# Second MLP product as seven products of quarter matrices in a two-layer streaming encoder

## The chip, the cores and the metric

The kernel runs on one core of a Trainium2 chip. The metric is the device time of one execution in microseconds (us).

## The reference

Input and output are 1024 tokens of 1024 channels, float32. Two layers; each is a token mixer (differential attention in layer 0, a gated linear recurrence in layer 1) and an MLP with squared ReLU, both behind an RMSNorm and added to the residual; a last RMSNorm ends the trunk.

```python
def rmsnorm(x, g, eps=NORM_EPS):
    y = x * lax.rsqrt(jnp.mean(x * x, axis=-1, keepdims=True) + eps)
    return y * g

def sqrelu_mlp(h, w1, w2):
    return jnp.square(jax.nn.relu(h @ w1)) @ w2

for layer in range(DEPTH):
    ...
    x = x + sqrelu_mlp(rmsnorm(x, mlp_norm_g[layer]), mlp_w1[layer], mlp_w2[layer])
return rmsnorm(x, final_norm_g)
```

`w1` is 1024 x 4096, `w2` 4096 x 1024 (`D_FF` = 4096).

## The kernel before, in words

Activations lie with channels on the partitions and tokens along the free axis (tiles of 128 x 1024, two halves of `CH` = 512 tokens); there are 8 such blocks of `x`. Each factor of a product is split into a high part (fp32r, a copy on ScalarE) and a low part (the difference, on VectorE or GpSimd, in `split`, L91), and each product is three matmuls: high by high, high by low, low by high, of 128 x 128 weights by 512 columns (`mm3`, `gemm_steps`, `hidden_pair`).

**First MLP product.** `mlp` runs 16 times `hidden_pair`, each for two blocks of 128 hidden channels (`ct`, top, and `cl`, low). A pair is one step of Strassen's scheme as changed by Winograd: seven products A11·B11, A12·B21, S2·T2, S3·T3, S1·T1, S4·B22, A22·T4, each 4 x 3 = 12 matmuls, 84 in all. The sums of token and channel blocks (T1 to T4 and the parts of x) are split once ahead; those of the weights (`s12`, `s34`) in `pair_weights`, one pair ahead: three high parts (`wth`, `wsh` twice) and a half one (`wl`) on ScalarE, the low ones on VectorE (`wsl`, `wl`) and GpSimd (`wtl`, L91). The seven results lie in seven PSUM banks (`acb`; `acg` twice; two tiles `acc` of two banks each, tag S with two buffers) and VectorE adds them up (L808, `mt`, `ct`, `cl`). `finish` multiplies both blocks by 1/rms on GpSimd (L840), applies relu and square on ScalarE and stores the block in DRAM (`hid`). It runs one pair later. The 1/rms comes from the sum of squares `ssacc` (`norm_later`; its columns are made in pair 1, since the norm is only applied to the product).

**Second MLP product.** `mlp` then walks `GROUPS`, five groups of 4, 8, 8, 8 and 4 hidden blocks. A group loads and splits its blocks (`hidden_load`) and weights (`w_out`), and `out_group` multiplies them into each of the 8 output blocks and adds the result to the residual `x` (L739). That is 32 hidden blocks x 8 x 2 halves x 3 = 1536 matmuls in a layer. In layer 1 the last group is `final_group`: tokens as rows, `x` transposed on TensorE (64 of them, L908), final norm and output.

The order of the instructions on each engine is set by the scheduler of the language, from the order of the code and its own estimates; the buffers (`BUFS`: 46 of tag T, 4 of R and W) bound how far it may reach.

Of the kernel before, what the change touches and what calls it, by code (L numbers as in the profile page):

```python
# [9 lines left out]
F32 = mybir.dt.float32  # L10
# [31 lines left out]
class Trunk:  # L42
    def __init__(self, ctx, tc, ins, out):
# [9 lines left out]
        self.w_lo = None  # L53

# [250 lines left out]
    def gemm_steps(self, w, xs, sel, evict, tag=None):  # L305
# [456 lines left out]
    def pair_weights(self, w1, i):  # L762
# [9 lines left out]
        th, tl = self.split(top, (P, NK, P), "wt", "W" if i else "T", lo_eng=nc.gpsimd)  # L772
# [7 lines left out]
        h12, l12 = self.split(s12, (P, NK, P), "ws")  # L780
# [5 lines left out]
    def hidden_pair(self, w, i, rb, before):  # L786
# [7 lines left out]
        steps = (("A11", "B11"), ("A12", "B21"), ("S2", "T2"), ("S3", "T3"), ("S1", "T1"), ("S4", "B22"), ("A22", "T4"))  # L794
# [3 lines left out]
        banks = (p1, p2, p67[:, l], p67[:, r], p53[:, l], p53[:, r], p4)  # L798

        def product(n, k, first, last):  # L800
            a, b = steps[n]
            (ah, al), (bh, bl) = w[a], self.sx[k][b]
            mm(banks[n], ah[:, k], bh, start=first, stop=False)  # L803
            mm(banks[n], ah[:, k], bl, start=False, stop=False)  # L804
            mm(banks[n], al[:, k], bh, start=False, stop=last)  # L805
# [4 lines left out]
        t = self.t4("mt")  # L810
        top, low = self.t4("ct"), self.t4("cl")
        u2, u3 = t[:, l], t[:, r]

        def done(n):
            if n == 0:
                nc.scalar.activation(out=u2, in_=p1, func=AF.Copy)
            elif n == 1:
                add(top[:, l], u2, p2)
            elif n == 2:
                add(u2, u2, banks[2])  # L820
            elif n == 3:
# [9 lines left out]
        for n in range(7):
            for k in range(4):
                product(n, k, k == 0, k == 3)
            done(n)
            if n in before:
                before[n]()

        def finish():
# [16 lines left out]
    def mlp(self, layer, done, last):  # L855
# [5 lines left out]
        for i in range(16):  # L861
# [9 lines left out]
            if i:  # L871
                finish()
# [297 lines left out]
```

## Time and profile before

| | us |
|---|---|
| median of 3 runs (2367.36 to 2368.62) | 2368.48 |
| profiled execution | 2370.26 |
| its span | 2368.5 |
| TensorE busy | 2231.6 (94%) |
| VectorE busy | 1390.9 (59%) |
| ScalarE busy | 955.5 (40%) |
| GpSimd busy | 531.8 (22%) |

The granted clock over the span is 0.974 of full speed. A matmul's busy time is its whole passage, so 884 of them in 200 us stand as 200 us of busy time. The first product of layer 0 lies at about 640 to 970 us of the span, its second product up to some 1320, then the recurrence; layer 1's MLP fills the span from about 1680 on.

### The profile page before, as it was taken

What the parts mean: (1) busy time and instruction counts of PE and PEld (TensorE: products, weight loads), DVE (VectorE), ACT (ScalarE), POOL (GpSimd) and SP (SyncE); (2) the same over time, 40 slices, a digit from 0 to 9 for tenths busy, and PEclk for the clock granted to TensorE, in tenths of its full rate; (3) what the DMA queues carried; (4) which work ended last, traced back from release to release, by engine and by line L of the source; (5) the groups of instructions that cost most, each with busy time, mean ns of one, the idle gap of its engine ahead of it and who ended that gap; (6) DMA issues with size and microseconds to landing.
All of it is one profiled execution on the core that took longest, in us unless ns stands there. A gap on an engine that the chain in (4) does not pass through costs nothing.

```text
span 2368.5 us, 26083 instructions
## 1 busy us (share of the span) xinstructions
PE 2231.6 (94%) x10206; PEld 1838.3 (78%) x10206; DVE 1390.9 (59%) x1639; ACT 955.5 (40%) x1466; POOL 531.8 (22%) x323
## 2 busy tenths in 40 slices
PE   8998889788979999999999998989699999999998
PEld 7776777676768888888888877867588888888887
DVE  5327667665877777632223576778967777422224
ACT  5225556464544444421111354554444444311114
POOL 3011112110345444511100000001544445301000
PEclk9999999998989999999999999989899999999999
DMA  6434445643513333743321111113133335633211
GB/s 192 132 89 111 107 111 126 176 114 91 188 63 115 108 115 107 252 139 98 98 63 49 59 42 30 45 45 107 45 98 115 108 107 174 220 104 95 78 51 72
DMA packets 222525, 250.92 MB, mean 106 GB/s; under 512 B 10209, under 2 KB 180290, under 8 KB 222402
## 3 DMA queue, kind: packets, MB, share of 16 engines
q1 hardware_dynamic: 213570, 221.99, 29.3%
q0 software_dynamic: 7680, 25.17, 4.6%
q8 instruction: 80, 1.31, 0.2%
q10 hardware_dynamic: 1152, 2.10, 0.2%
q14 instruction: 43, 0.35, 0.0%
HBM read 157.99 MB, written 57.67 MB: 91 GB/s over the span
## 4 chain that ended last, share of the span: by engine, by line
PE 60%; DVE 7%; ACT 3%; issue 1%; POOLq 0%; ACTq 0%; DVEq 0%
PE acc L325 8%; PE acc L326 8%; PE acc L328 7%; PE acc L803 5%; PE acc L804 5%; PE acc L805 5%; PE acg L328 3%; PE acg L326 3%; PE acg L325 3%; PE acg L803 2%; PE acg L804 2%; PE acg L805 2%; DVE t L255 1%; PE acb L804 1%; PE acb L805 1%
## 5 line engine op out<-in xcount | busy, mean ns | idle before, releaser
L325 PE MATMUL acc<-hh,woh 128*128 128x512 f32 x648 | 252.1, 389 | 0.0
L326 PE MATMUL acc<-hl,woh 128*128 128x512 f32 x648 | 252.1, 389 | 0.0
L739 DVE TENSOR_TENSOR x<-x,acc 128x1024 f32<-128x1024 f32 x69 | 83.8, 1216 | 236.1 <-PE acc L328 236.0
L328 PE MATMUL acc<-hh,wol 128*128 128x512 f32 x648 | 199.5, 389 | 0.0
L88 ACT ACTIVATE woh<-raw 128x1024 fp32r<-128x1024 f32 x76 | 80.4, 1058 | 278.2 <-PE acc L326 187.8
L91 POOL TENSOR_TENSOR wtl<-raw,wth 128x1024 fp32r<-128x1024 f32 x32 | 89.0, 2783 | 322.7 <-ACT wth L88 314.1
L91 POOL TENSOR_TENSOR hl<-raw,hh 128x1024 fp32r<-128x1024 f32 x32 | 81.4, 2546 | 348.4 <-ACT hh L88 348.3
L482 ACT ACTIVATE p<-acc,nmax 128x768 f32<-128x768 f32 (+7 forms) x128 | 95.3, 744 | 153.9 <-DVE nmax L499 56.4
L88 ACT ACTIVATE hh<-raw 128x1024 fp32r<-128x1024 f32 x64 | 66.6, 1056 | 188.9 <-DMA raw<-hid 178.2
L328 PEld LDWEIGHTS acc<-hh,wol 128*128 128x128 f32 x648 | 121.6, 188 | 25.4
L325 PEld LDWEIGHTS acc<-hh,woh 128*128 128x128 f32 x648 | 121.6, 188 | 25.2
L326 PEld LDWEIGHTS acc<-hl,woh 128*128 128x128 f32 x648 | 121.6, 188 | 25.2
L840 POOL TENSOR_TENSOR ct<-ct,rstdb 128x1024 f32<-128x1024 f32 x32 | 106.6, 3333 | 128.7 <-DVE ct L808 100.3
L325 PE MATMUL acg<-xgh,wh 128*128 128x512 f32 x320 | 135.3, 423 | 0.0
L840 POOL TENSOR_TENSOR cl<-cl,rstdb 128x1024 f32<-128x1024 f32 x32 | 88.8, 2774 | 178.0 <-DVE cl L808 109.1
L164 POOL TENSOR_TENSOR rstd<-ms,mhalf 128x4 f32<-128x4 f32 (+2 forms) x27 | 28.3, 1047 | 444.5 <-DVE ms L162 423.4
L328 PE MATMUL acg<-xgh,wl 128*128 128x512 f32 x320 | 127.7, 399 | 0.4 <-DVE wl L91 0.4
L326 PE MATMUL acg<-xgl,wh 128*128 128x512 f32 x320 | 127.2, 398 | 0.0
L325 PE MATMUL acg<-hh,woh 128*128 128x512 f32 x312 | 121.4, 389 | 0.0
L328 PE MATMUL acg<-hh,wol 128*128 128x512 f32 x312 | 121.4, 389 | 0.0
L326 PE MATMUL acg<-hl,woh 128*128 128x512 f32 x312 | 121.4, 389 | 0.0
L91 DVE TENSOR_TENSOR wol<-raw,woh 128x1024 fp32r<-128x1024 f32 x76 | 101.3, 1333 | 29.5 <-ACT woh L88 29.5
(328 smaller groups left out, 5888.2 us busy)
## 6 DMA issues: line engine op xcount, KB each, us to landing
raw<-in_mlp_w_dram SPq DMA_DIRECT2D x128, 512.0 KB, 4.2
raw<-hid SPq DMA_DIRECT2D x64, 512.0 KB, 3.3
x<-x SPq DMA_DIRECT2D x32, 512.0 KB, 5.0
hid<-ct SPq DMA_DIRECT2D x32, 512.0 KB, 2.6
hid<-cl SPq DMA_DIRECT2D x32, 512.0 KB, 8.2
raw<-in_attn_w_qkv_dram SPq DMA_DIRECT2D x24, 512.0 KB, 4.2
ks<-qkh POOLq DMA_DIRECT2D x32, 256.0 KB, 6.4
ks<-qkl POOLq DMA_DIRECT2D x32, 256.0 KB, 6.5
```

The costliest lines, as they stand in the source:

```text
L88: nc.scalar.activation(out=hi, in_=src, func=AF.Copy)
L91: (lo_eng or nc.vector).tensor_tensor(out=lo, in0=src, in1=hi.bitcast(F32), op=ALU.subtract)
L164: nc.gpsimd.tensor_tensor(out=r, in0=ms, in1=self.mhalf[:, :w], op=ALU.pow)
L325: mm(ps[:, pc], a, xh[:, cs], start=(k == 0), stop=False)
L326: mm(ps[:, pc], a, xl[:, cs], start=False, stop=False)
L328: mm(ps[:, pc], b, xh[:, cs], start=False, stop=(k == n - 1))
L482: nc.scalar.activation(out=p[c][:, :n], in_=src, func=AF.Exp, bias=nmax[:, c : c + 1], accum_out=sums[:, c : c + 1])
L739: nc.vector.tensor_tensor(out=self.x[m][:, cs], in0=self.x[m][:, cs], in1=ps, op=ALU.add)
L803: mm(banks[n], ah[:, k], bh, start=first, stop=False)
L804: mm(banks[n], ah[:, k], bl, start=False, stop=False)
L805: mm(banks[n], al[:, k], bh, start=False, stop=last)
L840: nc.gpsimd.tensor_tensor(out=c, in0=c, in1=rb(), op=ALU.mult)
```

## The change

The second product also becomes one Strassen step. The hidden matrix and `w2` are taken as 2 x 2 quarters; there are seven products of quarters, and each is accumulated in PSUM over its whole length of 16 hidden blocks (`second`). It is written as 56 slots of 24 matmuls: 8 P, 16 A, 16 B, 8 C and 8 D, 1344 matmuls in a layer. A and B slots work on two products at once. `load` runs `AHEAD` = 4 slots before use, `prepare` (the splits and the sums of weights) one slot before, `after` reads finished banks, and `side` holds steps of VectorE that are spread over later slots. The order on TensorE, ScalarE, VectorE and the DMA queue is that of the code there (`manual_schedule`).

`hidden_pair` takes its seven products in another order, keeps the sums in `ct` and `cl` without `mt`, and makes the four half-block sums that the second product needs (`h12`, `h34`, L840 of the new file) on VectorE; a pair stores seven half-blocks in DRAM. The factor 1/rms leaves the hidden blocks: since relu and square follow, its square (1/(mean + eps), `inv`) multiplies the result. `wtl` moves from GpSimd to VectorE. In layer 1 `turn_x` transposes `x` in pairs 3 to 10, tokens are rows in the whole second product, and `final_part` does the last norm half by half.

```diff
-        th, tl = self.split(top, (P, NK, P), "wt", "W" if i else "T", lo_eng=nc.gpsimd)
...
+        th, tl = self.split(top, (P, NK, P), "wt", hi_tag="W")
...
-        steps = (("A11", "B11"), ("A12", "B21"), ("S2", "T2"), ("S3", "T3"), ("S1", "T1"), ("S4", "B22"), ("A22", "T4"))
...
-            for c in (top, low):
-                nc.gpsimd.tensor_tensor(out=c, in0=c, in1=rb(), op=ALU.mult)
...
+        product("A11", "B11", p1)
+        nc.scalar.activation(out=top[:, l], in_=p1, func=AF.Copy)
+        product("S2", "T2", p67[:, l])
+        add(low[:, l], top[:, l], p67[:, l])
+        product("S1", "T1", p53[:, l])
+        add(low[:, r], low[:, l], p53[:, l])
+        product("S4", "B22", p53[:, r])
+        add(top[:, r], low[:, r], p53[:, r])
+        product("S3", "T3", p67[:, r])
+        both = low.rearrange("p (h c) -> p h c", c=CH)
+        add(both, both, p67[:, None, r].to_broadcast([P, 2, CH]))
+        product("A12", "B21", p2)
+        add(top[:, l], top[:, l], p2)
+        product("A22", "T4", p4)
+        add(low[:, l], low[:, l], p4, ALU.subtract)
...
+        for c in (top, low):
+            nc.scalar.activation(out=c, in_=c, func=AF.Relu)
+            nc.scalar.activation(out=c, in_=c, func=AF.Square)
...
+        if last:
+            two(a12[:, 0], top[:, r], low[:, r], ALU.add)
+            two(a12[:, 1], a12[:, 0], top[:, l])
+            two(a34[:, 0], top[:, l], top[:, r])
+            two(a34[:, 1], low[:, l], a12[:, 1])
+            put(3, a34[:, 1])
+            put(6, low[:, r])
+        else:
+            two(a12[:, 0], top[:, r], top[:, l])
+            two(a12[:, 1], low[:, r], a12[:, 0])
+            two(a34[:, 0], low[:, r], top[:, r])
+            two(a34[:, 1], low[:, l], a12[:, 1])
+            put(3, low[:, r])
+            put(6, a34[:, 1])
+        put(slice(1, 3), a12)
+        put(4, a34[:, 0])
...
+        ps = self.acc2()
+        for k in range(NT):
+            nc.tensor.transpose(ps[:, k * P : (k + 1) * P], t[:, k * P : (k + 1) * P], self.ident)
+        kept = self.t4("xk", F32, (P, NT, P))
+        nc.scalar.activation(out=kept, in_=ps.rearrange("p (k c) -> p k c", c=P), func=AF.Copy)
+        nc.sync.dma_start(out=self.xN.rearrange("(t p) c -> p t c", p=P)[:, :, m * P : (m + 1) * P], in_=kept)
...
+                inv = self.const.tile([P, NT], F32, name=f"inv{layer}")
+                nc.vector.tensor_scalar(out=inv, in0=ps[:, :NT], scalar1=1.0 / D, scalar2=EPS, op0=ALU.mult, op1=ALU.add)
+                nc.vector.reciprocal(out=inv, in_=inv)
+            if i == 3 and not last:
+                inv = self.spread(inv)
+            if last and 3 <= i < 3 + NK:
+                self.turn_x(i - 3)
+            self.hidden_pair(now, i, last)
...
+        slots = [("P", (2 * j, 2 * j + 1)) for j in range(8)]
+        slots += [("A", (i, i)) for i in range(16)] + [("B", (i, i)) for i in range(16)]
+        slots += [(c, (2 * j, 2 * j + 1)) for c in "CD" for j in range(8)]
...
+            xh, xl = self.split(xf, (P, 2, CH), "h2")
+            if kind == "A":
+                if i % 2 == 0:
+                    kept[i // 2] = self.t4("s2", F32, (P, 2, CH))
+                k = kept[i // 2][:, i % 2]
+                if last:
+                    tt(wf[:, 0], wf[:, 1], wf[:, 0])
+                    tt(k, side, wf[:, 0])
+                else:
+                    t = wf[:, 1]
+                    tt(t, t, side, ALU.add)
+                    tt(k, t, wf[:, 0])
+                wh, wl = self.t4("w2h", F32R, (P, 2, CH)), self.t4("w2l", F32R, (P, 2, CH))
+                first = wf[:, 0] if last else wf[:, 1]
+                nc.scalar.activation(out=wh[:, 0], in_=first, func=AF.Copy)
+                nc.scalar.activation(out=wh[:, 1], in_=k, func=AF.Copy)
+                tt(wl[:, 0], first, wh[:, 0].bitcast(F32))
+                tt(wl[:, 1], k, wh[:, 1].bitcast(F32))
             else:
...
+                if kind == "B" and last:
+                    tt(wf[:, 1], wf[:, 0], side)
+                elif kind == "B":
+                    tt(wf[:, 0], wf[:, 0], kept[i // 2][:, i % 2])
+                    tt(wf[:, 1], side[:, 0], side[:, 1])
+                elif kind == "D" and last:
+                    tt(wf, wf, kept[i // 2])
+                wh, wl = self.split(wf, (P, 2, CH), "w2")
+            parts[s] = wh, wl, xh, xl
...
+                by = lambda out, half: tt(out, out, inv[:, half], ALU.mult)
+                steps = (lambda: add(y12, y21, y22), lambda: by(y12, r), lambda: add(y22, y12, x(m + 4, r)), lambda: add(y12, y12, x(m, r)),
+                         lambda: by(y21, l), lambda: add(y21, y21, x(m + 4, l)), lambda: by(y11, l), lambda: add(y11, y11, x(m, l)))
...
+            for m, half in parts:
+                t = self.t4("xq", F32, (P, CH))
+                tt(t, bank, inv[:, half], ALU.mult)
+                terms.append((c[m][:, half], t))
+            return lambda: [tt(y, y, t, ALU.add) for y, t in terms]
...
+            elif kind == "B" and n == 0:
+                assert not side
+                for m in M4:
+                    fn = more(z[m], (m, r))
+                    side.append(lambda m=m, fn=fn: complete(m, r, fn))
+            elif kind == "B":
+                for m in M4:
+                    fn = more(u[m], (m + 4, r), (m + 4, l))
+                    side.append(lambda m=m, fn=fn: complete(m + 4, r, fn))
...
+        AHEAD = 4
+        for s in range(AHEAD):
+            load(s)
+        prepare(0)
+        for s in range(N - TAIL_SLOTS):
+            if s + AHEAD < N:
+                load(s + AHEAD)
+            prepare(s + 1)
+            kind, pairs = slots[s]
+            for n in range(2):
+                products(s, n)
+                if pairs[n] == 15:
+                    after(kind, n)
+            del parts[s]
+            for fn in side[: 3 if kind in "AB" else 2]:
+                if fn:
+                    fn()
+            del side[: 3 if kind in "AB" else 2]
+        tail = range(N - TAIL_SLOTS, N)
+        for s in tail[1:]:
+            prepare(s)
+        for fn in side:
+            fn()
+        for m in M4:
+            for s in tail:
+                for n in range(2):
+                    products(s, n, (m,))
+            complete(m + 4, l, more(u[m], (m + 4, l)))
...
+        nc.scalar.activation(out=sq, in_=x[:, cs], func=AF.Square, accum_out=ss[:, h : h + 1])
+        nc.vector.tensor_tensor(out=y[:, cs], in0=x[:, cs], in1=self.gb[:, cs], op=ALU.mult)
+        if h:
+            return
+        st = self.sm("fst", 1)
+        nc.vector.tensor_tensor(out=st, in0=ss[:, 0:1], in1=ss[:, 1:2], op=ALU.add)
+        r = self.rsqrt_small(st, 1.0 / D, EPS, 1)
+        ts = slice(t * P, (t + 1) * P)
+        nc.vector.tensor_scalar(out=y[:, :CH], in0=y[:, :CH], scalar1=r, scalar2=None, op0=ALU.mult)
```

**VectorE, a steady pair of layer 0's first product.** Before, from the last sums of pair i on (`s12`, `s34` and `wl` belong to the weights of the pair ahead, `mt`, `ct`, `cl` to the results):

```order
L808 TENSOR_TENSOR cl_1005_5949<-mt_1003_5947,acc_1002_5946 128x512
L808 TENSOR_TENSOR cl_1005_5949<-mt_1003_5947,acg_1000_5944 128x512
L771 TENSOR_TENSOR s12_1012_6088<-raw_1011_6086 128x512
L771 TENSOR_TENSOR s34_1013_6089<-raw_1010_6084,raw_1011_6086 128x512
L779 TENSOR_TENSOR wl_1016_6098<-raw_1011_6086,wl_1016_6098 128x512
L771 TENSOR_TENSOR s12_1012_6088<-s12_1012_6088,raw_1010_6084 128x512
L771 TENSOR_TENSOR s34_1013_6089<-raw_1010_6084,s12_1012_6088 128x512
L91 TENSOR_TENSOR wsl_1018_6102<-s12_1012_6088,wsh_1017_6101 128x1024
L808 TENSOR_TENSOR ct_1004_5948<-ct_1004_5948,acc_1002_5946 128x512
L91 TENSOR_TENSOR wsl_1020_6106<-s34_1013_6089,wsh_1019_6105 128x1024
L808 TENSOR_TENSOR ct_1027_6115<-mt_1026_6114,acg_1022_6110 128x512
L808 TENSOR_TENSOR mt_1026_6114<-mt_1026_6114,acc_1024_6112 128x512 x2
```

After, over the same stretch, up to the first sum of the next pair (the last row):

```order
L840 TENSOR_TENSOR h12_1230_7596<-cl_1229_7500,h12_1230_7596 128x512
L840 TENSOR_TENSOR h34_1231_7597<-cl_1229_7500,ct_1228_7499 128x512
L779 TENSOR_TENSOR s12_1234_7612<-raw_1233_7610 128x512
L779 TENSOR_TENSOR s34_1235_7613<-raw_1232_7608,raw_1233_7610 128x512
L92 TENSOR_TENSOR wtl_1237_7619<-raw_1232_7608,wth_1236_7618 128x1024
L840 TENSOR_TENSOR h34_1231_7597<-cl_1229_7500,h12_1230_7596 128x512
L787 TENSOR_TENSOR wl_1238_7622<-raw_1233_7610,wl_1238_7622 128x512
L779 TENSOR_TENSOR s12_1234_7612<-s12_1234_7612,raw_1232_7608 128x512
L779 TENSOR_TENSOR s34_1235_7613<-raw_1232_7608,s12_1234_7612 128x512
L92 TENSOR_TENSOR wsl_1240_7626<-s12_1234_7612,wsh_1239_7625 128x1024
L92 TENSOR_TENSOR wsl_1242_7630<-s34_1235_7613,wsh_1241_7629 128x1024
L814 TENSOR_TENSOR cl_1249_7639<-ct_1248_7638,acc_1246_7636 128x512
```

`wtl` and the half-block sums (`h12`, `h34`) stand among the weights' sums now, and no drain of the next pair stands ahead of the two `wsl`.

**TensorE, a pair of layer 1 with a transpose**, after (`wl` is A22, `wth`/`wtl` A11 and A12, `t12h` with `wsh` S1 or S2; `acc_2203` is the tile of the transposes, `acc_2208` and `acc_2209` those of the pair; in brackets the engines or queues waited for):

```order
L811 MATMUL acg_2206_13545<-b2h_2054_12586,wtl_2173_13363 128x512
L809 MATMUL acg_2207_13546<-t34h_2018_12427,wl_2174_13366 128x512 [waits DVE_49]
...
L811 MATMUL acg_2207_13546<-t34h_2058_12594,wl_2174_13366 128x512
L811 MATMUL acb_2228_13697<-b11_2013_12416,wtl_2196_13516 128x512 [waits DVE_49]
L809 MATMUL acb_2228_13697<-b11_2025_12469,wth_2195_13515 128x512
...
L874 MATMUL acc_2203_13532<-ident_72,xm_2202_13530 128x128 [waits DMAHW7_49]
L874 MATMUL acc_2203_13532<-ident_72,xm_2202_13530 128x128 x7
L809 MATMUL acc_2208_13547<-t12h_2016_12423,wsh_2175_13369 128x512 [waits PE_49]
...
L809 MATMUL acc_2209_13548<-t12h_2016_12423,wsh_2175_13369 128x512 [waits Activation_49]
```

Between A11 and S2·T2 stand the eight transposes; before, no transpose stood in the first product, all 64 in `final_group`.

**VectorE, layer 0's second product.** Before, two consecutive stretches of `out_group` (`hl`, `wol`: low halves of hidden blocks and weights, `x`: sum into the residual):

```order
L739 TENSOR_TENSOR x_1297_8057<-x_1297_8057,acc_1309_8105 128x1024
L91 TENSOR_TENSOR hl_1338_8306<-raw_1336_8303,hh_1337_8305 128x1024
L739 TENSOR_TENSOR x_1302_8091<-x_1302_8091,acg_1314_8139 128x512
L739 TENSOR_TENSOR x_1302_8091<-x_1302_8091,acg_1315_8140 128x512
L91 TENSOR_TENSOR wol_1333_8248<-raw_1331_8245,woh_1332_8247 128x1024
L739 TENSOR_TENSOR x_1310_8131<-x_1310_8131,acc_1323_8181 128x1024
L91 TENSOR_TENSOR hl_1352_8430<-raw_1350_8427,hh_1351_8429 128x1024
L739 TENSOR_TENSOR x_1316_8167<-x_1316_8167,acc_1327_8213 128x1024
```

After, two B slots (`h2l`, `w2`, `w2l`: split and sums of the slot ahead; `x`: side steps):

```order
L922 TENSOR_TENSOR w2_1461_8944<-w2_1461_8944,s2_1368_8401 128x512
L922 TENSOR_TENSOR w2_1461_8944<-w3_1463_8947 128x512
L92 TENSOR_TENSOR w2l_1500_9109<-w2_1461_8944,w2h_1499_9108 128x1024
L922 TENSOR_TENSOR x_1475_9014<-x_1352_8341,xr_1480_9040 128x512
L922 TENSOR_TENSOR x_1352_8341<-x_1352_8341,xr_1479_9038 128x512
L922 TENSOR_TENSOR x_1475_9014<-x_1475_9014,rstdb_1040_6230 128x512
L92 TENSOR_TENSOR h2l_1505_9146<-h2_1469_8987,h2h_1504_9145 128x1024
L922 TENSOR_TENSOR w2_1468_8986<-w2_1468_8986,s2_1368_8401 128x512
L922 TENSOR_TENSOR w2_1468_8986<-w3_1470_8989 128x512
L92 TENSOR_TENSOR w2l_1507_9152<-w2_1468_8986,w2h_1506_9151 128x1024
L922 TENSOR_TENSOR x_1475_9014<-x_1475_9014,xr_1482_9044 128x512
```

A slot holds the split, two sums of weight blocks and two or three side steps, each slot in the same order.

## Rows read from the trace of the kernel before

**Rows 1.** the page: busy time of each engine, and shares of the chain that ended last

```profile
PE 2231.6 (94%) x10206; PEld 1838.3 (78%) x10206; DVE 1390.9 (59%) x1639; ACT 955.5 (40%) x1466; POOL 531.8 (22%) x323
...
PE 60%; DVE 7%; ACT 3%; issue 1%; POOLq 0%; ACTq 0%; DVEq 0%
```

**Rows 2.** windows: busy us (instructions) by engine, clock, DMA share, GB/s; 200 us in both MLPs

```profile
800.00:1000.00 200.00, 200.00 (x884) 165.62 (x883) 144.35 (x142) 90.49 (x98) 96.53 (x33) 1.00 0.43 146
...
2000.00:2200.00 200.00, 200.00 (x884) 165.62 (x883) 71.60 (x64) 52.22 (x50) 39.41 (x16) 1.00 0.45 149
```

**Rows 3.** windows of 20 us where the first product hands over to the second

```profile
980.00:1000.00 20.00, 20.00 (x90) 16.57 (x89) 10.63 (x10) 11.43 (x12) 11.42 (x4) 1.00 0.96 353
2000.00:2020.00 20.00, 20.00 (x90) 16.57 (x89) 10.68 (x10) 9.55 (x10) 13.31 (x5) 1.00 0.95 350
```

**Rows 4.** timeline of VectorE, one pair: start, us, instruction, idle before and releaser

```profile
789.48 0.69 DVE L808 TENSOR_TENSOR ct<-mt,acc 128x512 f32<-128x512 f32 x1 [1.63 <-PE acc L805]
792.43 0.69 DVE L808 TENSOR_TENSOR mt<-mt,acc 128x512 f32<-128x512 f32 x1 [2.26 <-PE acc L805]
...
794.35 0.68 DVE L771 TENSOR_TENSOR s<-raw 128x512 f32<-128x512 f32 x1
794.96 2.89 DVE L771 TENSOR_TENSOR s<-raw,raw 128x512 f32<-128x512 f32 x1
...
800.58 0.68 DVE L771 TENSOR_TENSOR s<-s,raw 128x512 f32<-128x512 f32 x1
801.29 0.69 DVE L771 TENSOR_TENSOR s<-raw,s 128x512 f32<-128x512 f32 x1
802.39 1.23 DVE L91 TENSOR_TENSOR wsl<-s,wsh 128x1024 fp32r<-128x1024 f32 x1 [0.40 <-ACT wsh L88]
803.53 0.68 DVE L808 TENSOR_TENSOR ct<-ct,acc 128x512 f32<-128x512 f32 x1
...
808.52 0.69 DVE L808 TENSOR_TENSOR ct<-mt,acc 128x512 f32<-128x512 f32 x1 [1.63 <-PE acc L805]
```

**Rows 5.** windows, entry of the MLP of layer 0

```profile
660.00:680.00 20.00, 12.53 (x37) 9.28 (x38) 20.00 (x14) 8.17 (x10) 14.30 (x6) 0.66 0.07 27
```

**Rows 6.** timeline of ScalarE: independent copies, then relu and square

```profile
649.85 1.04 ACT L88 ACTIVATE t34h<-t 128x1024 fp32r<-128x1024 f32 x1
650.79 1.04 ACT L88 ACTIVATE wth<-raw 128x1024 fp32r<-128x1024 f32 x1
...
711.03 1.06 ACT L842 ACTIVATE ct<-ct 128x1024 f32<-128x1024 f32 x1 [2.56 <-POOL ct L840]
712.12 1.06 ACT L843 ACTIVATE ct<-ct 128x1024 f32<-128x1024 f32 x1
```

**Rows 7.** timeline in the recurrence: one VectorE instruction, then two of TensorE

```profile
1371.31 1.22 DVE L91 TENSOR_TENSOR xbl<-xb,xbh 128x1024 fp32r<-128x1024 f32 x1 [1.18 <-ACT xbh L88]
...
1371.33 0.50 PE L325 MATMUL acc<-xbh,wgh 128*128 128x512 f32 x1 [1.58 <-ACT xbh L88]
...
1432.64 1.22 PE L325 MATMUL acc<-xbh,wgh 128*128 128x512 f32 x2 [4.67 <-ACT xbh L88]
```

**Rows 8.** timeline of GpSimd in the same pair

```profile
794.57 2.73 POOL L840 TENSOR_TENSOR cl<-cl,rstdb 128x1024 f32<-128x1024 f32 x1 [5.84 <-issue]
```

**Rows 9.** groups of instructions by line, 2280 to 2368 us: the transposes

```profile
L908 PE MATMUL acg<-ident,x 128*128 128x128 f32 x64 | 8.9, 272 | 0.0
```

**Rows 10.** the page: GpSimd's power

```profile
L164 POOL TENSOR_TENSOR rstd<-ms,mhalf 128x4 f32<-128x4 f32 (+2 forms) x27 | 28.3, 1047 | 444.5 <-DVE ms L162 423.4
```

**Rows 11.** windows of 2 us around two idle times of TensorE

```profile
1370.00:1372.00 2.00, 0.67 (x3) 0.48 (x3) 0.82 (x2) 1.06 (x1) 0.00 (x0) 1.00 0.80 243
...
1432.00:1434.00 2.00, 1.33 (x3) 0.61 (x3) 1.39 (x2) 0.58 (x1) 0.00 (x0) 0.50 0.00 0
...
1436.00:1438.00 2.00, 2.00 (x6) 1.52 (x6) 1.23 (x1) 1.97 (x3) 0.00 (x0) 0.50 0.04 8
1438.00:1440.00 2.00, 2.00 (x9) 1.65 (x8) 0.28 (x1) 1.99 (x3) 0.00 (x0) 0.85 0.00 0
```

More of the change, by code (lines that the diff above doesn't have):

```diff
@@ L53, in __init__ @@
         self.w_lo = None
+        self.late_first = False
     def t4(self, name, dt=F32, shape=(P, 1024), tag="T"):
@@ L318, in gemm_steps @@
         else:
-            groups = [(self.accg(), slice(half * CH, (half + 1) * CH)) for half in range(2)]
+            groups = [(self.accg(), slice(half * CH, (half + 1) * CH)) for half in ((1, 0) if self.late_first else (0, 1))]
+            self.late_first = False
         for ps, span in groups:
@@ L797, in hidden_pair, with product @@
         l, r = slice(0, CH), slice(CH, S)
[L798 to L805, printed above, removed]
+        def product(a, b, bank):
+            for k in range(4):
+                (ah, al), (bh, bl) = w[a], self.sx[k][b]
+                mm(bank, ah[:, k], bh, start=k == 0, stop=False)
+                mm(bank, ah[:, k], bl, start=False, stop=False)
+                mm(bank, al[:, k], bh, start=False, stop=k == 3)
@@ L831, in hidden_pair @@
[L831 to L838, printed above, removed]
-            for c in (top, low):
-                nc.gpsimd.tensor_tensor(out=c, in0=c, in1=rb(), op=ALU.mult)
-            for c, b in ((top, i), (low, i + 16)):
-                nc.scalar.activation(out=c, in_=c, func=AF.Relu)
-                nc.scalar.activation(out=c, in_=c, func=AF.Square)
-                nc.sync.dma_start(out=self.hid[b], in_=c)
@@ new lines, in hidden_pair, with two @@
+        a12, a34 = self.t4("h12", F32, (P, 2, CH)), self.t4("h34", F32, (P, 2, CH))
+        def two(out, x, y, op=ALU.subtract):
+            nc.vector.tensor_tensor(out=out, in0=x, in1=y, op=op)
+        f = self.hid[i]
+        put = lambda at, src: nc.sync.dma_start(out=f[:, at], in_=src)
+        put(0, top[:, l])
+        put(5, low[:, l])
+        if last:
[12 more added lines that the diff above has]
+            put(6, a34[:, 1])
@@ L856, in mlp @@
+    def mlp(self, layer, last):
         nc = self.nc
         w1, w2 = self.ins["mlp_w1"][layer], self.ins["mlp_w2"][layer]
-        rb = self.norm_later()
-        self.hid = [self.dram.tile([P, S], F32, name=f"hid{layer}_{b}") for b in range(DFF // P)]
-        hs = []
+        ssacc = self.ssacc
+        self.hid = [self.dram.tile([P, 7, CH], F32, name=f"hid{layer}_{b}") for b in range(16)]
+        if last:
+            self.xN = self.dram.tile([S, D], F32, name="xN")
         for i in range(16):
@@ L864, in mlp @@
                 self.w = self.pair_weights(w1, i + 1)
-            else:
-                for b in range(GROUPS[0][0], sum(GROUPS[0])):
-                    self.hidden_load(hs, b)
-                first = self.w_out(w2, GROUPS[0][0] * P, GROUPS[0][1], 0)
-            before = {RB_AT[0]: rb.columns, RB_AT[1]: finish} if i == 1 else {}
-            finish = self.hidden_pair(now, i, rb, before)
-            if i:
-                finish()
-        self.x = []
-        def load_x(n):
-            for m in range(len(self.x), min(n, NK)):
-                self.x.append(self.t4("x"))
-                nc.sync.dma_start(out=self.x[m], in_=self.xD[m])
@@ new lines, in mlp @@
+            if i == 2:
+                ps = self.acc1()
+                for j in range(NT):
+                    nc.tensor.matmul(ps[:, j : j + 1], ssacc[:, j * P : (j + 1) * P], self.ones, start=True, stop=True)
+                inv = self.const.tile([P, NT], F32, name=f"inv{layer}")
[3 more added lines that the diff above has]
+                inv = self.spread(inv)
```

265 lines of the change are left out of this document (166 added, 99 removed).

## The prediction, on record before the changed kernel ran

> **What bounds the kernel now.** I read the page first, for shares, then windows over the two MLPs, for the price of a matmul and for what the transfers can do, then the timelines of VectorE and ScalarE, for the duration of each kind of instruction, and last the windows and the timeline around the idle times of TensorE, for the clock. The page has TensorE busy for 94% of the span, and TensorE alone makes up 60% of the chain that ended last [rows 1]. In both MLPs nothing stands in its way: 884 matmuls in every 200 us, no idle time, clock 1.00, or **0.2262 us a matmul** [rows 2]. That holds where one product hands over to the other [rows 3]. So matmuls taken out there come off the span one for one, and any new wait of TensorE is added one for one. VectorE's half-idle share (59%) hides that its order matters: in one pair of the first product it has 1.63 and 2.26 us to spare, in 19.04 us from one start to the next [rows 4].
>
> **What the change takes out.** The second product falls from 1536 to 1344 matmuls a layer, the first keeps 1344. 2 x 192 x 0.2262 = **-86.9 us**. The order of TensorE's instructions confirms it (404 fewer matmul instructions in all, 20 of them small ones outside the two products), so a change that does not do what it says is ruled out. The 64 transposes of the old last group are now in layer 1's first product: no gain. At the entry of each MLP GpSimd's weight halves are gone; TensorE ran 37 matmuls in 20 us there, where 88 would fit, with VectorE full [rows 5]. I take back 2 us a layer (-4; between 0 and -10).
>
> **Durations.** A 512-wide VectorE operation costs 0.60 us from start to start (0.61 in the row), 0.71 if it needs the one before it, a 1024-wide one 1.14 [rows 4]. ScalarE: 0.95 for 1024 columns, 1.09 dependent [rows 6]. A round trip VectorE, ScalarE, VectorE leaves VectorE idle for 1.18 [rows 7]. In the old pair a 512-wide operation took 2.89 instead of 0.68, and the one behind it as much, while GpSimd worked on the same stretch [rows 4, 8]. In the new MLP GpSimd has no work, so I take 0.60; were the 2.89 not GpSimd's doing, two of them in 32 pairs would add up to 2 x 2.2 x 32 = 141. The Trainium skill, SBUF — State Buffer, section "Who interferes with whom", says that a VectorE instruction with two SBUF inputs is blocked by a GpSimd one that reads SBUF; by that rule they go back to 0.68, and the sum is the one below.
>
> **First product: a longer chain.** VectorE now also makes the lower weight half (1.14) and four half-block sums (2.4), and these wait for relu and square. Set t = 0 where S4·B22 of pair j ends on TensorE. VectorE drains it (0.77), adds S3·T3 to both halves (2.03) and subtracts A22·T4 (2.72). ScalarE relu-squares `ct` until 2.93 and `cl` until 5.0. VectorE's h12 runs at 2.97; the next h12 waits for the square of `cl` (5.04) and holds up all that stands behind it: h34, s12, s34 (start 5.64, 6.24, 6.84), wtl (7.44), h34, wl (8.58, 9.18), s12, s34 (9.78, 10.50), wsl after ScalarE's wsh (11.6), the second wsl after wth and wsh (13.5), and only then the first drain of the next pair (14.66 to 15.35). TensorE may begin S3·T3 only when that drain is over, and has 60 matmuls in between: it is there at about 13.7. From 15.4 it runs S3·T3 and S4·B22, 24 matmuls, 5.43. The period is 20.85 against 19.0: +1.85 a pair. Layer 0, 14 steady pairs: **+26**. Layer 1, six pairs without a transpose: **+11**.
>
> The eight pairs of layer 1 with `turn_x` are worse. There TensorE's order is A22·T4 (waits for the last drain, 2.72), A11's lower half (waits for wtl, 8.6; TensorE is there at 5.4), 8 transposes, S2·T2, S1·T1. S1·T1 needs a PSUM tile that ScalarE's copy of the last pair's transposes frees, behind wsh (14.4); with 10 matmuls, the transposes (0.14 each [rows 9]) and S2·T2, TensorE comes to it at 14.8. From there 47 matmuls (10.6): 25.4 against 20.1 for a pair of 84 matmuls and 8 transposes. 8 x 5.3 = **+42**. In both kinds of pair the bounds are nothing, if the drain is over in time, and for the second another 2 us a pair, if ScalarE comes later to its copy.
>
> **Entry into the second product.** TensorE has nothing left when the last pair's matmuls end: drain and relu-square (5.1), h2h and w2h (7.1), three half-block sums, h2l, w2l: 8.9 in layer 0, 9.7 in layer 1, where before the windows are full [rows 3]. **+18.6** (bounds: 2 x 5.1, the drain and relu-square alone, and 2 x 12, if each split waits for its turn).
>
> **Second product, slot by slot.** A slot is 24 matmuls, 5.43. P costs VectorE 2.3 and A 3.85: covered by TensorE, which pays if they rise above 5.43. B in layer 0 costs h2l 1.14, two sums 0.60 and 0.68, the round trip 1.18, w2l 1.14 = 4.7, and with three side steps (1.9) 6.6: 1.2 over, in the 13 slots that have side steps (two only in some): **+10.7**; layer 1 without the second sum: +0.5. Behind the last B stand 12 products with the squared 1/rms, then the completed blocks (add, ScalarE, low half, sum of squares, 2.6 each), all ahead of the next slot's split. By the same adding up the first C slots of layer 0 are late by 7.6, 3.0, 3.7 and 0.5 (**+14.8**), D by 2.1 and 2.4 (**+4.6**), C in layer 1 by 1.8. In layer 1's D slots the final rms goes through GpSimd's power (1.05 [rows 10]), some 2.95 a block; D1 is late by 5.3, D2 by 5.1, and the tail needs four slots split first: 8.3. **+18.8.** Entered together: 11.2 + 21.2 + 18.8 = +51.2.
>
> **Transfers.** A B slot of layer 0 asks for 1.57 MB in 5.43 us, 290 GB/s; 350 has been carried [rows 3], and loads run four slots ahead. Nothing taken; a late load would be paid in full, one or two us a slot over 16 slots at worst.
>
> **The clock.** After 1.58 us without a matmul the clock stayed at 1.00 (2.4 GHz); after 4.67 it fell to 0.50 (1.2 GHz) for 6 us and was 0.85 on average in the 2 us after [rows 7, 11], which costs 3.0 + 0.3 = 3.3 us. Four new gaps are longer than that one (8.9, 9.7, 7.6, 8.3): **+13**. The largest of a transpose pair (5.4 to 8.6) lies between the two: 0 or 8 x 3.3 = 26; I take 0, as no single gap there reaches 4.67.
>
> **Sum.** -86.9 - 4 + 26 + 11 + 42 + 18.6 + 51.2 + 13 = **+71**. The profiled execution took 2370.3, 1.8 over the median of the runs; 2368.5 + 71 = 2439.5, say **2440**.
>
> **The rivals.**
> 1. *The chain of the first product fits after all* (faster). It decides at 13.7 us: were the drain of the next pair over before TensorE reaches S3·T3, the 26 and 11 would vanish, and with them most of the 42, which hangs on the same chain. Then 71 - 79 = -8: 2360. For it: the margin in plain pairs is only 1.7 us in a chain of 18 operations. Against it: every duration is a row, the order is fixed, and in the transposed pairs the waits sum up to three times that. 0.15.
> 2. *The second product keeps TensorE fed*: its splits run ahead enough that the B, C and D terms go, with two of the four clock falls. 71 - 51 - 7 = +13 alone, 2381; together with rival 1 -66, 2302. For it: TensorE lags too, which gives VectorE room. Against it: prepare stands only one slot ahead, and a loss is made up on neither engine. 0.16, of which 0.10 with rival 1, since the same few durations would have to be shorter in both.
> 3. *Gaps make further gaps through the clock*: the clock falls in each transpose pair (+26), and B's loads come late (+10): 2475. For it: [rows 11] show the fall after one gap. Against it: no gap in between has been seen. 0.14. The Trainium skill, TensorE: Matmul & The Clock Gate, section "Why this matters for your kernels", warns of idle gaps between bursts of matmuls that send the array back to the half clock; by that rule the time is this rival's, and the row of 4.67 us agrees with it while that of 1.58 does not decide.
>
> **How the numbers follow.** Forecast (2415 to 2462): 0.55. Rival 3: 0.14. Rival 1: 0.15. Rival 2: 0.10 beside rival 1 and 0.06 alone. What a measurement can tell from no change is about 0.2%, 4.7 us: 2364 to 2373. Faster is both rivals together (0.10) and most of rival 1 (0.13): 0.23. Same is the rest of it and the lower end of rival 2: 0.03. Slower: 0.74. The range leaves out the joint case and the lower part of rival 1 below, and the end of rival 3 above: 2350 to 2485.
>
> **What would show it.** Right: in a steady pair of layer 0 TensorE waits about 1.8 us before S3·T3 for the drain into `cl`; pairs with transposes start some 25 us apart; VectorE has no idle time in B slots of layer 0 while TensorE has 1.2; gaps of 8 to 10 us at the two entries, with the clock at 0.50 behind them. Wrong: pairs 19 us apart (rival 1), B and C slots 5.43 apart (rival 2), or transposed pairs at 0.50 (rival 3).

## The result, and the profile after

| | before | after |
|---|---|---|
| median, us | 2368.55 | 2565.89 (2563.03 to 2568.24, 4 runs) |
| span of the profiled execution | 2368.5 | 2563.3 |

The ratio is 1.0832 (95% interval 1.0814 to 1.0851): **197 us slower**, where 71 slower was forecast and 2350 to 2485 was the range. The direction was right, the size was not. (A correction to the section on the kernel before: `finish` runs right behind its own pair; only pair 0's came a pair later.)

The page of the changed kernel, the lines that answer to [rows 1], and the granted clock in 40 slices:

```profile
PE 2239.3 (87%) x9794; PEld 1799.7 (70%) x9794; DVE 1578.4 (62%) x2069; ACT 1059.8 (41%) x1616; POOL 163.1 (6%) x193
...
PEclk9999999889899999999989899998988889999997
...
PE 35%; DVE 18%; ACT 11%; issue 6%; DMA 2%; SPq 0%; ACTq 0%; POOL 0%; DVEq 0%; POOLq 0%
```

TensorE's matmuls are fewer (9794 for 10206), but its busy share fell from 94 to 87%, and its share of the chain that ended last from 60 to 35: VectorE, ScalarE and a transfer now stand between its matmuls. Eleven slices of the clock row are below 9, where the kernel before had four. Two windows of the first product of layer 0 (columns as in [rows 2]):

```profile
860.00:880.00 20.00, 18.93 (x83) 15.34 (x83) 12.61 (x18) 8.09 (x9) 0.00 (x0) 1.00 0.39 132
900.00:920.00 20.00, 18.49 (x74) 14.67 (x73) 11.59 (x16) 5.71 (x7) 0.00 (x0) 0.91 0.33 112
```

Between 1825 and 2106 us lie the eight pairs of layer 1 with a transpose. The window over them, and below it one over the first product of layer 1 in the kernel before, where TensorE was full:

```profile
1825.00:2106.00 281.00, 196.55 (x764) 153.74 (x763) 112.48 (x147) 75.83 (x83) 0.00 (x0) 0.85 0.35 112
```

```profile
1740.00:2012.50 272.50, 272.50 (x1204) 225.65 (x1203) 205.28 (x198) 119.71 (x131) 131.38 (x44) 1.00 0.38 124
```

The eight pairs are a stretch of 281 us with 764 matmuls, 64 of them transposes, at a mean clock of 0.85; at 0.2262 us each that is 173 us of work at most. The waits of TensorE from 1780 to 2200 us (us in total, times, longest) name the cause:

```profile
PE acc L874 <- DMA xm<-x: 54.6, 8, 7.5
PE acb L811 <- DVE wtl L92: 15.2, 8, 2.9
PE acg L809 <- DVE cl L814: 14.5, 7, 2.1
```

The second and third are the two waits of the prediction (for `wtl`, 2.9, and for the last drain, 2.1). The first was not in it: some 7 us a pair for the load (`xm`) of the part of `x` that is to be transposed. SyncE's queue in one such pair (start, us, what is issued; each issue follows what it waits for):

```profile
1898.33 0.32 SPq L843 DMA_DIRECT2D hid<-ct  x1
1900.37 0.80 SPq L843 DMA_DIRECT2D hid<-cl  x2
1901.70 3.26 SPq L843 DMA_DIRECT2D hid<-h  x2
1905.25 0.38 SPq L64 DMA_DIRECT2D raw<-in_mlp_w_dram  x1
1906.45 0.32 SPq L843 DMA_DIRECT2D hid<-h  x1
1907.05 0.38 SPq L64 DMA_DIRECT2D raw<-in_mlp_w_dram  x1
1907.54 1.09 SPq L871 DMA_DIRECT2D xm<-x  x1
```

The load of `xm` goes out last, behind the stores of `ct`, `cl` and the half-block sums `h`, each of which waits for its producer. TensorE's timeline in the same pair, every instruction that waited:

```profile
1879.42 1.97 PE L874 MATMUL acc<-ident,xm 128*128 128x128 f32 x8 [6.15 <-DMA xm<-x]
...
1898.16 0.50 PE L809 MATMUL acg<-t34h,wl 128*128 128x512 f32 x1 [2.08 <-DVE cl L814]
...
1904.07 0.51 PE L811 MATMUL acb<-b,wtl 128*128 128x512 f32 x1 [1.68 <-DVE wtl L92]
...
1913.70 1.97 PE L874 MATMUL acc<-ident,xm 128*128 128x128 f32 x8 [7.03 <-DMA xm<-x]
```

The load goes out at 1907.54, TensorE has been idle since 1906.67, and the transposes start at 1913.70. From one pair's transposes to the next it is 34.3 us.

### The profile page after: what moved, and what is told of

Read it like the earlier page. It is cut to its first block, busy times and chain, and to the rows that moved or that the text cites. A ratio compares the mean times of both kernels' runs of the same rounds, so it can differ in the third digit from the quotient of the medians.

```text
span 2563.3 us, 26499 instructions
## 1 busy us (share of the span) xinstructions
PE 2239.3 (87%) x9794; PEld 1799.7 (70%) x9794; DVE 1578.4 (62%) x2069; ACT 1059.8 (41%) x1616; POOL 163.1 (6%) x193
## 4 chain that ended last, share of the span: by engine, by line
PE 35%; DVE 18%; ACT 11%; issue 6%; DMA 2%; SPq 0%; ACTq 0%; POOL 0%; DVEq 0%; POOLq 0%
PE acc L809 3%; PE acc L1009 3%; PE acc L1008 3%; PE acc L1007 3%; PE acc L811 3%; PE acc L810 3%; DVE s L779 3%; DMA xm<-x 2%; DVE wtl L92 1%; DVE h L840 1%; PE acc L333 1%; ACT cl L836 1%; ACT cl L835 1%; PE acb L1009 1%; PE acb L1008 1%
## 5 line engine op out<-in xcount | busy, mean ns | idle before, releaser
L92 DVE TENSOR_TENSOR h2l<-h,h2h 128x1024 fp32r<-128x1024 f32 x112 | 136.9, 1222 | 68.8 <-ACT h2h L89 68.1
L89 ACT ACTIVATE h2h<-h 128x1024 fp32r<-128x1024 f32 x112 | 117.3, 1047 | 29.4 <-DMA h<-hid 28.5
L1007 PE MATMUL acc<-w2h,h2h 128*128 128x512 f32 x256 | 105.4, 412 | 19.9 <-ACT w2h L89 11.3
L1007 PE MATMUL acc<-h2h,w2h 128*128 128x512 f32 x256 | 101.5, 396 | 8.1 <-DVE h L840 6.9
L1008 PE MATMUL acc<-w2l,h2h 128*128 128x512 f32 x256 | 104.8, 409 | 4.3 <-DVE w2l L92 4.3
L809 PE MATMUL acc<-t12h,wsh 128*128 128x512 f32 x256 | 104.3, 410 | 0.1
L1009 PE MATMUL acc<-w2h,h2l 128*128 128x512 f32 x256 | 103.9, 406 | 0.0
L810 PE MATMUL acc<-t12l,wsh 128*128 128x512 f32 x256 | 103.4, 404 | 0.0
L1009 PE MATMUL acc<-h2h,w2l 128*128 128x512 f32 x256 | 101.7, 397 | 1.5 <-DVE w2l L92 1.5
L811 PE MATMUL acc<-t12h,wsl 128*128 128x512 f32 x256 | 102.9, 402 | 0.0
```

Of the source, the lines that this page charges most:

```text
L89: nc.scalar.activation(out=hi, in_=src, func=AF.Copy)
L92: (lo_eng or nc.vector).tensor_tensor(out=lo, in0=src, in1=hi.bitcast(F32), op=ALU.subtract)
L809: mm(bank, ah[:, k], bh, start=k == 0, stop=False)
L810: mm(bank, ah[:, k], bl, start=False, stop=False)
L811: mm(bank, al[:, k], bh, start=False, stop=k == 3)
L1007: mm(bank[m], ah, bh, start=first, stop=False)
```

## The experiments

All are compared with the kernel before on the same chip, which ran at 2368.7 to 2369.7; "less" is the distance to the change's 2565.9. Eleven kernels ran.

**1. The load of x on another queue.**

```diff
-        nc.sync.dma_start(out=t, in_=self.xD[m])
+        nc.gpsimd.dma_start(out=t, in_=self.xD[m])
```

> The load of x for the transposes is issued on GpSimd's DMA queue, which has nothing else in the MLP, instead of SyncE's; the order on TensorE, VectorE and ScalarE is the same as in the changed kernel. Theory (the load stands in SyncE's queue behind the stores of the pair's half-blocks, which wait for relu, square and the sums): TensorE's 54.6 us of waits for xm go, and with them half-clock time; the eight pairs come down from 34 us to the 25.4 of the prediction: 2490 to 2510 against 2566. Rival (the pair is bound by the PSUM tile that ScalarE's copy frees, and the load is only the last of several): the wait moves to S1T1 or the copy, 2545 or more.

Measured: **2500.0** (ratio 1.0551, 1.0520 to 1.0583), 66 less than the change. TensorE's waits from 1780 to 2150 us in this kernel:

```profile
PE acb L811 <- DVE wtl L92: 19.9, 8, 2.9
PE acg L809 <- DVE cl L814: 14.6, 7, 2.1
```

No wait for `xm` is left; the two foreseen ones stay. The load now goes out early (at 1877.55 in the pair that the first line below marks), and it lands after 3.6 us, where it took 6.2 on SyncE's queue. VectorE's drain behind S4·B22, the mark of a pair, comes at these times:

```profile
1877.06 0.69 DVE L814 TENSOR_TENSOR ct<-cl,acc 128x512 f32<-128x512 f32 x1 [7.25 <-PE acc L811]
...
1902.55 0.69 DVE L814 TENSOR_TENSOR ct<-cl,acc 128x512 f32<-128x512 f32 x1 [7.25 <-PE acc L811]
...
1930.96 0.69 DVE L814 TENSOR_TENSOR ct<-cl,acc 128x512 f32<-128x512 f32 x1 [7.25 <-PE acc L811]
...
1956.44 0.69 DVE L814 TENSOR_TENSOR ct<-cl,acc 128x512 f32<-128x512 f32 x1 [7.24 <-PE acc L811]
```

These are 25.5, 28.4 and 25.5 us apart; the other five of the eight are 27.1. The window over all eight:

```profile
1822.85:2037.70 214.85, 180.32 (x746) 143.45 (x745) 109.87 (x144) 72.65 (x80) 4.41 (x8) 0.93 0.46 147
```

That is 26.9 us a pair, against 34.6 in the changed kernel and 25.4 in the prediction. A clock of 0.93 over 214.85 us is some 15 us lost, and it is below 1.00 in each of the eight: 27.1 us at a mean clock of 0.94 are 25.4 and 1.6 lost to the clock. The pairs of 25.5 meet the forecast by luck: the half clock lies ahead of the wait for `wtl` there, which is then 1.3 us instead of 2.9. So the queue that was left out makes up most of the difference, and the clock the rest.

**2. No transposes.** They are left out; `xN` gets `x` as it is.

```diff
     def turn_x(self, m):
...
+        self.nc.gpsimd.dma_start(out=self.xN[m * P : (m + 1) * P], in_=self.xD[m])
```

> Leaves out the 64 transposes with their PSUM tiles and copies: xN is filled with x as it is, by a transfer on GpSimd's queue. Theory (all that layer 1's first product loses beyond layer 0's is turn_x): eight pairs at 20.9 instead of 34: 2455 to 2475. Rival (layer 1's own order of the half-block sums costs as well): 2480 to 2510, with plain pairs longer than in layer 0.

Measured: **2458.5** (1.0376, 1.0339 to 1.0413), 107 less than the change, as expected: `turn_x` was the larger part of layer 1's loss, and without it the pairs are 21.2 or 22.7 us apart, as in layer 0.

**3. The sums one pair later.**

```diff
+        def finish():
+            a12, a34 = self.t4("h12", F32, (P, 2, CH)), self.t4("h34", F32, (P, 2, CH))
...
+        return finish
...
-            self.hidden_pair(now, i, last)
+            finish, now = self.hidden_pair(now, i, last), finish
+            if now:
+                now()
```

> The four half-block sums and the stores of a pair are issued one pair later, so that on VectorE they wait for no relu and square of the same pair. Theory (the drain into cl before S3T3 is late since the sums hold up the weights' operations): plain pairs fall from 20.8 to 19.0, 20 pairs and their half-clock stretches: 2515 to 2540. Rival (VectorE's amount of work, not its order, sets the pair): 2555 to 2575.

Measured: **2393.5** (1.0102, 1.0072 to 1.0131), 172 less than the change, where 26 to 51 were expected. A window of this kernel in layer 0, then one in the transposed pairs of layer 1:

```profile
800.00:820.00 20.00, 20.00 (x90) 16.57 (x89) 14.36 (x20) 9.50 (x10) 0.00 (x0) 1.00 0.46 151
```

```profile
1880.00:1900.00 20.00, 19.88 (x92) 16.41 (x91) 13.15 (x18) 8.92 (x11) 0.00 (x0) 1.00 0.60 197
```

TensorE is full with the same work on VectorE, so the order was the bound and not the amount. The expectation missed layer 1: there the sums held up not only the weights but also the stores, and behind those the load of `x`. That load is still on SyncE's queue here, and TensorE waits for it 0.3 us in all: it was its place in the queue that cost, not the queue.

**4. The first slot of the second product early.** The first two loads and the split of slot 0 stand before pair 15; the edit's other lines divide `second` at that place.

```diff
+            if i == 15:
+                second = self.second(w2, inv, last)
+                next(second)
...
         prepare(0)
+        yield
```

> The first two loads and the split of the first slot of the second product are issued before the last pair of the first product; the rest is as in the changed kernel. Theory (the gap of 6.9 us at each entry is the split of slot 0 queued behind the last pair's sums, and the clock falls behind it): both gaps go, 2 x (6.9 + 3): 2540 to 2550. Rival (slot 1 is just as late, behind the same sums): the gap moves one slot on, 2560 to 2568.

Measured: **2555.7** (1.0786, 1.0754 to 1.0819): 10 less, between the two. The waits of TensorE at the entries fell from 6.9 us to 2.5 in layer 0 and 3.6 in layer 1; 0.9 of each is for the last pair's drain, the rest almost all for the low halves of the first slots, which stand behind the last sums.

**5. Only the stores later.** The sums stay where the change has them.

```diff
-        put(0, top[:, l])
-        put(5, low[:, l])
...
+        def finish():
+            put(0, top[:, l])
+            put(5, low[:, l])
```

> Only the stores of a pair's half-blocks are issued one pair later; the four sums stay where the changed kernel has them. Theory (the 172 us that the later sums and stores gave have two causes, VectorE's order and SyncE's queue): this gives the queue's part alone, 2495 to 2515, with plain pairs still near 20.8. Rival (it was all the queue: stores that wait hold up the loads of weights and x): 2393 to 2430, with pairs at 19.

Measured: **2564.6** (1.0823, 1.0792 to 1.0855), no difference, and it decided nothing: the scheduler put the stores at the same places of SyncE's queue as before the edit. The load of `xm` was still waited for 49.4 us. So how much of the 172 us is VectorE's order and how much the queue's is not shown by it; experiment 1 is the one that moved the load.

**6 to 8. Three waits, each alone, on top of experiment 3** (2393.5). Splits three slots ahead:

```diff
-        AHEAD = 4
+        AHEAD, PREP = 6, 3
...
-            prepare(s + 1)
+            if s + PREP < N and s + PREP not in parts:
+                prepare(s + PREP)
...
```

> The kernel with the later sums, and in the second product the splits run three slots ahead of the products instead of one (loads six instead of four). Theory (VectorE has enough time over all slots; B, C and D lose only since it may not work ahead): the waits there go, 30 to 45 us of 2393: 2350 to 2365. Rival (VectorE's work at the end of B and in D is too much at once for three slots): 2375 to 2393, with waits of several us left at C and D.

Measured: **2357.4** (0.9949, 0.9927 to 0.9972): 36 less. Slots 0 and 1 split before the last pair:

```diff
-        prepare(0)
+        for s in range(2):
+            prepare(s)
+        yield
...
```

> The kernel with the later sums, and the first two slots of the second product are loaded and split before the last pair of the first. Theory (with one slot ahead the gap only moved to slot 1): both entry gaps with their half clock go, 2393 - 20: 2370 to 2377. Rival (the last sums and stores of hidden blocks 14 and 15 hold up slot 2 as well): 2383 or more.

Measured: **2378.0** (1.0038, 1.0022 to 1.0054): 15.5 less, 1 us outside what was expected. One slot early was not enough; with two a wait of 0.9 us is left at each entry. Pair 0's high halves out of tag W:

```diff
-        th, tl = self.split(top, (P, NK, P), "wt", hi_tag="W")
+        th, tl = self.split(top, (P, NK, P), "wt", hi_tag="W" if i else "T")
...
-        h12, l12 = self.split(s12, (P, NK, P), "ws", hi_tag="W")
+        h12, l12 = self.split(s12, (P, NK, P), "ws", hi_tag="W" if i else "T")
```

> The kernel with the later sums, and the high weight halves of pair 0, made near the end of the mixer, lie in tag T as in the kernel before, not in the four buffers of W. Theory (the recurrence is some 15 us longer since its own weights have only two of the four W buffers while those halves wait): its waits for woh go and 2393 falls to 2378 to 2386. Rival (the recurrence is longer since the hand-written order of the second product lets no recurrent weight be split ahead): 2390 to 2395, with the first waits, for xbh, unchanged.

Measured: **2369.1** (0.9999, 0.9988 to 1.0011): 24 less, more than expected. The waits of TensorE at the end of the attention, 560 to 740 us, in the kernel of experiment 3 and in this one:

```profile
PE acb L810 <- DVE b L269: 10.8, 3, 4.6
PE acc L333 <- ACT woh L89: 6.8, 3, 4.2
```

```profile
PE acb L810 <- DVE b L269: 2.6, 2, 1.4
...
PE acc L333 <- ACT woh L89: 0.9, 1, 0.9
```

The output weights (`woh`) share the four W buffers; two of them were held from the first split of pair 0 to the pair itself. The wait for the split of `x` (`b`) shrinks with it. VectorE drains S4·B22 of the first pair of layer 0 at 692.59 instead of 707.44, 14.9 of the 24 us; the rest is gained in the same way ahead of layer 1's first product. The waits for `xbh` in the recurrence, named by the rival, did stay (12.8 and 6.3 us before, 12.9 and 6.4 now).

**9 and 10. All of them, and a longer lead.** Experiment 9 has the edits of 3, 6, 7 and 8 (`AHEAD, PREP = 6, 3`), experiment 10 the same with `AHEAD, PREP = 8, 5`.

> The four edits together: sums and stores one pair later, splits three slots ahead, the first two slots before the last pair, pair 0's high halves in tag T. If they take away different waits (36, 15.5 and 24 us below 2393.5): 2315 to 2325, below the kernel before (2369). If they share waits, the early slots and the splits ahead above all: 2325 to 2345.

> As the kernel with all four edits, with the splits five slots ahead instead of three. If what is left at C and D is VectorE's lack of lead: 3 to 10 us below it. If it is buffers or the last slots, no difference within 2 us.

Measured: **2312.8** (0.9761, 0.9742 to 0.9779) and, with five slots of lead, **2306.0** (0.9733, 0.9717 to 0.9748). The four edits add up (172 + 36 + 15.5 + 24 = 248, and together 253), so each takes away another wait. Both beat the kernel before, the second by 63 us.

**11. The sums and stores later in layer 0 alone.**

> The sums and stores one pair later in layer 0 only; layer 1 as in the changed kernel. Theory (layer 0 loses by VectorE's order alone, 38 us with the half-clock stretches; the rest of the 172 us is layer 1's, where the load of x hangs on the same sums): 2522 to 2532. Rival (layer 0's later sums help the recurrence and layer 1 too): 2515 or less.

Measured: **2527.3** (1.0668, 1.0639 to 1.0696): 38.6 of the 172 us are layer 0's, which leaves 134 for layer 1.

## Why the prediction was right or wrong, point by point

**The gain, -86.9: the price held, 63 of it were reached.** With most of the waits gone, experiment 10 is 63 us below the kernel before, and its first products are full at the old price. By the starts of TensorE's matmuls its second products are some 32 and 30 us shorter than before, of 43.4 each. Windows of that kernel:

```profile
700.00:1000.00 300.00, 299.13 (x1327) 247.55 (x1325) 209.02 (x274) 134.97 (x144) 0.00 (x0) 1.00 0.50 171
1750.00:1950.00 200.00, 198.96 (x900) 164.16 (x901) 136.21 (x182) 92.95 (x101) 0.00 (x0) 1.00 0.54 179
```

**First product of layer 0, +26: mechanism right, size short.** The chain stands in the trace as it was written down. VectorE, one pair from 887.14 on, and above it the mark of the pair before (start, us, instruction, idle before):

```profile
866.00 0.69 DVE L814 TENSOR_TENSOR ct<-cl,acc 128x512 f32<-128x512 f32 x1 [4.46 <-PE acc L811]
...
887.14 0.69 DVE L814 TENSOR_TENSOR ct<-cl,acc 128x512 f32<-128x512 f32 x1 [4.46 <-PE acc L811]
...
890.05 0.69 DVE L840 TENSOR_TENSOR h<-ct 128x512 f32<-128x512 f32 x1 [0.25 <-ACT ct L836]
892.09 0.69 DVE L840 TENSOR_TENSOR h<-cl,h 128x512 f32<-128x512 f32 x1 [1.35 <-ACT cl L836]
...
893.91 0.68 DVE L779 TENSOR_TENSOR s<-raw,raw 128x512 f32<-128x512 f32 x1
...
898.72 1.23 DVE L92 TENSOR_TENSOR wsl<-s,wsh 128x1024 fp32r<-128x1024 f32 x1 [0.46 <-ACT wsh L89]
900.61 1.23 DVE L92 TENSOR_TENSOR wsl<-s,wsh 128x1024 fp32r<-128x1024 f32 x1 [0.67 <-ACT wsh L89]
901.75 0.68 DVE L814 TENSOR_TENSOR cl<-ct,acc 128x512 f32<-128x512 f32 x1
...
909.86 0.69 DVE L814 TENSOR_TENSOR ct<-cl,acc 128x512 f32<-128x512 f32 x1 [6.03 <-PE acc L811]
```

Set 887.09 to 0: the first h at 2.96 (2.97 was worked out), the second at 5.0 (5.04), the wsl at 11.6 and 13.5 (11.6, 13.5), the drain of the next pair at 14.66 (14.66). The operation that took 2.89 in the old kernel [rows 4] is at 0.68; its mean fell from 2477 ns to 684, and GpSimd is idle in these windows. The Trainium skill, SBUF — State Buffer, section "Who interferes with whom", says that a VectorE instruction with two SBUF inputs contends with a GpSimd one that reads SBUF; the traces agree. TensorE's wait before S3·T3 is shorter than the 1.8 us that were to show it (0.64), since 0.86 of it stand a little earlier: two matmuls of the next A11·B11 wait there for ScalarE's copy out of their bank, behind the same `wsh`.

What the sum had too small is the clock and two pairs. In the third and fourth pair TensorE waits 3.07 us for ScalarE's copy ahead of the matmuls that spread `inv` (the squared 1/rms) over the partitions, and 3.07 for ScalarE's copy of their result. The two pairs take 23.3 and 27.0 us, with falls of the clock, 10 us more together than in the kernel of experiment 3. Of the ten after them, those that keep the clock are 21.14 us apart (20.85 predicted), three 22.7. Windows in one of the three, and TensorE's waits at the end of the pair before (the first two lines) and in this one:

```profile
902.00:904.00 2.00, 1.51 (x5) 1.18 (x6) 1.72 (x3) 0.00 (x0) 0.00 (x0) 0.74 0.08 22
904.00:906.00 2.00, 2.00 (x6) 1.63 (x5) 0.00 (x0) 0.00 (x0) 0.00 (x0) 0.50 0.00 0
906.00:908.00 2.00, 2.00 (x9) 1.62 (x9) 0.00 (x0) 0.00 (x0) 0.00 (x0) 0.90 0.00 0
```

```profile
879.97 0.50 PE L809 MATMUL acb<-b,wth 128*128 128x512 f32 x1 [0.87 <-ACT ct L818]
881.35 0.50 PE L809 MATMUL acc<-t34h,wsh 128*128 128x512 f32 x1 [0.64 <-DVE cl L814]
...
901.12 0.50 PE L809 MATMUL acb<-b,wth 128*128 128x512 f32 x1 [0.86 <-ACT ct L818]
902.49 0.50 PE L809 MATMUL acc<-t34h,wsh 128*128 128x512 f32 x1 [0.64 <-DVE cl L814]
```

After the two gaps of 0.86 and 0.64 us the clock fell to 0.50 for some 3 us; after the same two in the pair before it stayed at 1.00:

```profile
882.00:886.00 4.00, 4.00 (x19) 3.30 (x18) 0.68 (x2) 0.00 (x0) 0.00 (x0) 1.00 0.02 4
```

"After 1.58 us without a matmul the clock stayed at 1.00" was the row that priced this at nothing. Experiment 11 puts the term at 38.6.

**First product of layer 1, +53: wrong, 134 measured (172 less 38.6). This is the step that failed.** The working took TensorE's waits from "the last drain", from `wtl` and from the PSUM tile that ScalarE's copy frees, and these came as foreseen or cost nothing; but it took the transposes' own input to be there. The prediction listed the orders of TensorE, VectorE and ScalarE and not SyncE's, where the load of `x` stands behind stores that wait for the very chain that it had worked out. Experiment 1 shows it: 66 us with that load on another queue, and pairs of 26.9 on average instead of 34.6, where 25.4 was said. The rest, 68 against 53, goes with the clock, which the prediction took at 0 for these pairs because "no single gap there reaches 4.67". Without the queue's wait it still fell in all eight (0.93 over them, some 15 us), with no gap over 2.9: rival 3, held to be less likely.

**Entries into the second product, +18.6 and half the clock term: about right.** TensorE's wait there in the changed kernel, 1020 to 1070 us:

```profile
PE acc L1007 <- DVE h L840: 6.9, 1, 6.9
```

It is 6.9 in both layers, where 8.9 and 9.7 were worked out: TensorE starts once the high halves are there and waits for the low ones one by one (0.4 and 0.3 us in layer 0). With the half clock behind them the entries cost 23.5 us in all, by the starts of the matmuls (25.2 said); removing them gave 15.5.

**Slots B, C, D and the tail, +51.2: right in kind, short in layer 1.** In layer 0's B slots VectorE is over its share by as much as was said (65.6 of 80 us busy, plus the round trips), and C begins late (columns as in [rows 2]):

```profile
1180.00:1260.00 80.00, 73.43 (x299) 54.16 (x298) 65.64 (x84) 24.25 (x25) 0.00 (x0) 1.00 0.63 221
```

```profile
1280.00:1300.00 20.00, 12.97 (x44) 9.81 (x45) 16.78 (x23) 10.67 (x16) 0.00 (x0) 0.74 0.27 98
```

The 80 us of B hold 299 matmuls where 354 would fit, 12.4 us less, against 10.7 in the sum for all of B. The wait at the first C slot was 6.8 us (7.6 worked out). By the starts of the matmuls, with the clock's part in it, all slots of both layers lose some 66 us, where 51.2 and 6.6 for two falls were said; layer 1's D slots and tail alone lose 27 (18.8 and 3.3 said). Three slots of lead took 36 us away, five 7 more.

**Transfers, nothing: right.** No wait of TensorE for a transfer stands in the second products.

**The entry of the MLPs, -4: wrong sign.** "GpSimd's weight halves are gone" was counted, the tag of the buffers was not. `hi_tag="W"` is a word in the diff and cost 24 us by experiment 8. By the starts of TensorE's matmuls, the changed kernel is 11 us later than the old one at the end of layer 0's first pair, and loses 12 more in the recurrence and at the entry of layer 1, +23 in all; an estimate from these two figures is that about -1 would be left without the tag.

**The sum.** In place of +26, +53 and -4 the runs gave 38.6, 134 and +24: 122 us, of the 126 that the forecast was short. The starts of TensorE's matmuls in the two traces give 39, 129 and +23 for the same stretches, and 7 us more than forecast in the second products. Rivals 1 and 2 fell: the chain did not fit, and the second product was not fed. Rival 3's clock did fall in every transposed pair, but without the queue its 2475 was still 91 us short.

## What to carry to other kernels

A queue of transfers is an engine with an order of its own: list what each load stands behind, as for VectorE, before calling it hidden. Sums that nobody needs soon should not stand, on an in-order engine, between work that is awaited and its own late inputs; one pair's delay was worth 172 us here with no change in the work. A new tag on a buffer is a change of its own: count who else lives in it.

## What was not expected of the hardware

TensorE's clock fell after two waits of 0.86 and 0.64 us, 1.4 us apart, in some pairs and not in others with the same waits (pairs of 21.14 and 22.7 us side by side), while one of 1.58 us in the kernel before left it at 1.00 [rows 7, 11]. The Trainium skill, TensorE: Matmul & The Clock Gate, section "A second HAM failure mode: psum-queue depth-cycling", says that frequent short idle times between groups of matmuls make the clock go down and up; these rows agree, but do not show what decides between the pairs. In the transposed pairs, with waits of 7.0 us, each transpose took 421 ns at the half clock, where 272 was its duration in the kernel before.
